# Small expert slots of a mixture of experts in plain float32, in two column tiles, alternating with full slots

## The chip, the cores and the metric

The kernel runs on one core of one Trainium2 chip. Its time is the device time of one execution in microseconds (us), a median over runs. A profile is one execution taken by the hardware profiler; its times count from the start of the profiled span. TensorE (PE) multiplies and transposes, with a separate stream of weight loads (PEld); VectorE (DVE), ScalarE (ACT) and GpSimd (POOL) work elementwise; SyncE (SP) issues the weight transfers.

## The reference

Two transformer blocks over 512 tokens of 1024 channels. The first is a state-space mixer followed by a mixture of 32 experts; the second is attention, a recurrence and a feed-forward layer. The change lies in the mixture:

```
logits = (tok @ w_router + b_router)
top_logit, top_idx = lax.top_k(logits, TOP_K)            # 4 of 32 experts a token
...
gu = xe @ w_gate_up[e] + b_gate_up[e]                    # [tokens, 1024] x [1024, 2048]
gate = jnp.minimum(gu[:, :D_FF], 7.0)
up = jnp.clip(gu[:, D_FF:], -7.0, 7.0)
act = (up + 1.0) * gate * jax.nn.sigmoid(1.702 * gate)
y = act @ w_down[e] + b_down[e]                          # [tokens, 1024] x [1024, 1024]
```

Each expert gets the tokens that chose it, 64 on average (512 x 4 / 32), and each result is weighted and added to its token's row. All is float32.

## The kernel before

The program runs `mixer`, then `moe` (L1168 to L1439), then `block2`. In `mixer`'s tail, `router` computes the choices, and sorts experts 2 to 31 by their number of tokens into 32 slots. A slot is one expert with a fixed room: 64 tokens (`HALF`, slots 2 to 13), 256 (`DOUBLE`, slots 14 and 23), or 128 (a full slot). Slots 0 and 1 hold experts 0 and 1. What no room covers would go to a loop for extra blocks at the end of `moe`.

The slots run in the order of their numbers. For each, `up` is the first product (eight raw buffers of 1 MB with 128 rows of weights each), `swiglu` the nonlinearity, and `down` the second product (four buffers). The second product of a slot runs after the first product of the next slot, so that the nonlinearity has time. `transposed` turns the tokens or hidden rows (L1233 on TensorE) and splits the result into two halves (L92).

A weight passes through three engines. SP loads it (`W.load`, or L1343 for the second product) into one of 13 raw buffers. `W.part` splits it, 1024 columns at a time: ScalarE casts it to a rounded upper half `whi` (L86), VectorE subtracts that for the lower half `wlo` (L87). TensorE multiplies three times (`mm3`, L99, L100, L101): upper by upper, lower by upper, upper by lower, all float32r. A raw buffer is free when the subtraction has read it.

A slot's tokens come by an indirect transfer that POOL issues (L1239), and its results leave by ScalarE's scaling (L1325, L1318 in a double slot), POOL's multiplication (L1326) and an indirect scatter that adds (L1327); the last slot uses VectorE (L1321) instead of the two.

Which instruction stands where on an engine is decided by a scheduler that simulates a timeline, and by explicit rules (`issue_after`). Each engine executes in that order.

Two other places matter for reading the trace. `mod_rest` (L515, in the mixer) multiplies raw weights in plain float32, four matmuls side by side in tiles of 32 array columns. L669 multiplies in plain float32 in tiles of 64 columns, first one and then the other.

Of the kernel before, what the change touches and what calls it, by code (L numbers as in the profile page):

```python
# [8 lines left out]
F32 = mybir.dt.float32  # L9
# [35 lines left out]
class Split:  # L45
    """Streams weights: raw float32 chunks, and exact float32r halves of their parts."""
# [50 lines left out]
def mm3(nc, out, a, b, first, last):  # L97
    """a, b: halves of the stationary and the moving operand"""
# [5 lines left out]
# pools whose buffers a new tile takes over without waiting for the neighbours  # L104
# [3 lines left out]
class Kernel:  # L108
# [12 lines left out]
    def behind(self, ins):  # L121
        """what is issued under this follows the given instructions on their engines"""
# [27 lines left out]
    def brow(self, pool, src, o, n, name):  # L150
        """a row of DRAM on every partition"""
# [4 lines left out]
    def rinv(self, out, src, scale, bias):  # L156
        """out = 1 / sqrt(src * scale + bias), wide"""
# [5 lines left out]
    def rsqrt(self, pool, out, src, scale, bias, n, eng=None):  # L163
        """out = 1 / sqrt(src * scale + bias) for [P, n] with a small n, by Newton's iteration"""
# [17 lines left out]
    def softplus(self, out, x, e, u, l, eng):  # L182
        """log(1 + exp(x)) = max(x, 0) + log1p(exp(-|x|)); e, u, l: scratch"""
# [6 lines left out]
        # where u rounds to 1, log1p(e) is e itself  # L190
# [8 lines left out]
    # ------------------------------------------------------------------ block 1: mixer  # L199
    def mixer(self):  # L200
# [38 lines left out]
        # --- normalised x and ctx, channels on partitions; modulation vectors  # L239
        with ExitStack() as s0:  # L240
# [50 lines left out]
            # x is turned while the modulation's weights come in  # L291
# [44 lines left out]
        # the convolution's silu is x' (1 + tanh x') with x' = x / 2  # L336
# [9 lines left out]
        def proj(raw, with_ctx, split=False):  # L346
            """psum tiles of 128 output columns; raw: weights, or their halves"""
# [10 lines left out]
        def decays(tp, px, pc, scr):  # L358
            """dt, and the decays of both directions: forward heads on 32 partitions, backward on the next"""
# [45 lines left out]
        # --- decays and Fourier mixing  # L405
# [57 lines left out]
        # x, then ctx, between zeros  # L463
# [7 lines left out]
        def tokens(x, b):  # L471
            """a block of 128 tokens of a convolution's output"""
# [20 lines left out]
        def gate(i):  # L493
            """two tiles of the gates (1 + tanh, twice the sigmoid): first of the Fourier path, then of the scan's"""
# [13 lines left out]
        def mod_rest(half):  # L508
            """rows of the modulation for the residual gates and the second norm"""
# [8 lines left out]
            def rows32(src, o, n):  # L518
                """512 columns on each 32 partitions"""
# [7 lines left out]
            if half == 0:  # L527
                # the mix is held twice as large
# [24 lines left out]
        def group_tables(B, C):  # L553
            """B with tokens on partitions, and the masked C B^T of the chunks"""
# [28 lines left out]
        # a pair of heads' own work is interleaved with the projections of the next pair  # L583
# [8 lines left out]
        for p in range(16):  # L592
# [4 lines left out]
            # x with tokens on partitions, weighted by dt and by dt * decay to the chunk's end  # L597
# [15 lines left out]
            # decays within the chunks  # L613
# [19 lines left out]
            # chunk states, carried forward and backward  # L633
# [30 lines left out]
            # within the chunks  # L664
# [7 lines left out]
            # from the states before the chunks  # L672
# [28 lines left out]
            # projections of the next group, gates, rows of the modulation  # L701
# [28 lines left out]
        # the mix, by halves of the tokens  # L730
# [5 lines left out]
        # the logits are those of x1 / rms: with the second norm's weights in the router's, its shift in the bias  # L736
# [75 lines left out]
    def bias_parts(self, src, dst):  # L812
        """three bfloat16 parts, whose sum is src, of all experts' biases: on 32 partitions each"""
# [59 lines left out]
    def recurrence_constants(self, tp):  # L873
        """half of 8 log sigmoid(lambda) and all of it, and half the biases of the gates"""
# [10 lines left out]
    # ------------------------------------------------------------------ block 1: mixture of experts  # L885
    def router(self, mx, keep, xT, ahead, st, stp):
        """The mixer's output projection, h2 and the choices of experts. keep: a pool that outlives this."""
# [10 lines left out]
        # first, for the experts' tokens come to lie here  # L898
# [23 lines left out]
        def normed(b, pw, c):  # L922
            """x1 and h2 of a block"""
# [48 lines left out]
        def picked(b):  # L972
            """the first expert's tokens, transposed, are taken from h2 by a product"""
# [194 lines left out]
    def moe(self, mx):  # L1168
# [162 lines left out]
        def act_T(act):  # L1331
            return transposed(act, 1.0 / 1.702)
# [657 lines left out]
```

## Time and profile before

| what | value |
|---|---|
| median of 3 runs | 3072.28 us (3068.34 to 3073.09) |
| span of the profiled execution | 3071.3 us |
| TensorE busy | 2964.1 us (97%) |
| VectorE busy | 2292.2 us (75%) |
| ScalarE busy | 1738.8 us (57%) |
| mean DMA rate | 210 GB/s |

The profiled execution's own time is given only as its span. Busy means that an instruction of that engine is running. The stretches of the mixture were cut at the first matmul of certain slots: slots 0 and 1, then twelve small ones, a double with its two followers, six full, a double with two, five full, and the last slot.

### The profile page before, as it was taken

The numbers are of one execution on the slowest core, as the hardware profiler recorded it, in microseconds if no ns is written. First come the engines' busy times: TensorE is split into PE (matmuls) and PEld (weight loads), VectorE is DVE, ScalarE is ACT, GpSimd is POOL, SyncE is SP. The second block draws the span as 40 slices with busy tenths as digits, with TensorE's granted clock in tenths as the row PEclk, the third lists the DMA queues.
The fourth block names the chain that finished last, engine by engine and source line by source line (L and its number), as shares of the span: only waits on it lengthen the run. The fifth ranks groups of instructions, "written<-read, shape, count | busy, mean of one in ns | idle before, by whom it ended". The sixth has DMA issues, their size and how long they took to land. (4 is left out here: it accounts for less than half of the span.)

```text
span 3071.3 us, 40680 instructions
## 1 busy us (share of the span) xinstructions
PE 2964.1 (97%) x15088; PEld 2319.1 (76%) x15088; DVE 2292.2 (75%) x2968; ACT 1738.8 (57%) x2288; POOL 431.2 (14%) x375
## 2 busy tenths in 40 slices
PE   5999999999998999999999999999969999999999
PEld 3888888788776655555677787777768888788887
DVE  4637877787769999999789997899967777843322
ACT  4444545455444777777567775677745666632221
POOL 1211121122112111111021110211130000100000
PEclk9999999999998999999999999999989999999999
DMA  8244373644747898999779997799742212443331
GB/s 217 87 121 120 107 223 127 208 139 126 216 185 289 315 344 336 342 347 347 264 258 363 367 353 252 293 369 363 264 135 79 79 52 83 158 110 96 96 103 62
DMA packets 302602, 644.62 MB, mean 210 GB/s; under 512 B 18849, under 2 KB 190513, under 8 KB 268640
## 3 DMA queue, kind: packets, MB, share of 16 engines
q1 hardware_dynamic: 275744, 569.77, 52.1%
q0 software_dynamic: 24672, 67.93, 8.2%
q10 hardware_dynamic: 1984, 4.28, 0.4%
q8 instruction: 120, 1.97, 0.3%
q14 instruction: 82, 0.67, 0.1%
HBM read 618.85 MB, written 35.21 MB: 213 GB/s over the span
## 5 line engine op out<-in xcount | busy, mean ns | idle before, releaser
L87 DVE TENSOR_TENSOR wlo<-wraw,whi 128x1024 fp32r<-128x1024 f32 x1016 | 1274.4, 1277 | 439.1 <-ACT whi L86 426.2
L86 ACT CAST whi<-wraw 128x1024 fp32r<-128x1024 f32 (+1 forms) x1019 | 1058.5, 1046 | 791.7 <-PE pg L101 231.3
L99 PE MATMUL px<-hThi,whi 128*128 128x512 f32 x576 | 231.6, 404 | 0.0
L101 PE MATMUL px<-hThi,wlo 128*128 128x512 f32 x576 | 227.3, 395 | 2.5 <-DVE wlo L87 2.5
L100 PE MATMUL px<-hTlo,whi 128*128 128x512 f32 x576 | 228.0, 396 | 0.0
L1326 POOL TENSOR_TENSOR y<-y,g2b 128x1024 f32<-128x1024 f32 (+1 forms) x33 | 87.4, 2652 | 945.2 <-ACT y L1325 864.5
L100 PE MATMUL pg<-wlo,T0h 128*128 128x512 f32 (+1 forms) x416 | 167.7, 403 | 2.9 <-DVE wlo L87 2.2
L99 PE MATMUL pg<-whi,T0h 128*128 128x512 f32 (+1 forms) x416 | 165.3, 397 | 0.0
L101 PE MATMUL pg<-whi,T0l 128*128 128x512 f32 (+1 forms) x416 | 163.9, 394 | 0.0
L100 PE MATMUL pg<-wlo,T2h 128*128 128x512 f32 (+1 forms) x352 | 141.9, 403 | 1.6 <-DVE wlo L87 1.1
L100 PE MATMUL pf<-hnlo,whi 128*128 128x512 f32 (+1 forms) x384 | 142.4, 372 | 0.0
L101 PE MATMUL pf<-hnhi,wlo 128*128 128x512 f32 (+1 forms) x384 | 142.4, 372 | 0.0
L99 PE MATMUL pf<-hnhi,whi 128*128 128x512 f32 (+1 forms) x384 | 141.6, 372 | 0.0
L99 PE MATMUL pg<-whi,T2h 128*128 128x512 f32 (+1 forms) x352 | 139.6, 397 | 0.0
L484 DVE SCALAR_TENSOR_TENSOR cacc<-cr,vecs,cacc 128x770 f32<-128x770 f32 (+1 forms) x128 | 121.4, 957 | 23.1 <-ACT cacc L482 21.9
L101 PE MATMUL pg<-whi,T2l 128*128 128x512 f32 (+1 forms) x352 | 138.3, 393 | 0.0
L101 PEld LDWEIGHTS px<-hThi,wlo 128*128 128x128 f32 x576 | 109.1, 189 | 28.6 <-DVE wlo L87 3.7
L100 PE MATMUL pg<-wlo,T1h 128*128 128x512 f32 (+1 forms) x320 | 129.7, 405 | 0.8
L99 PE MATMUL pg<-whi,T1h 128*128 128x512 f32 (+1 forms) x320 | 127.7, 399 | 0.0
L101 PE MATMUL pg<-whi,T1l 128*128 128x512 f32 (+1 forms) x320 | 126.7, 396 | 0.0
L99 PEld LDWEIGHTS px<-hThi,whi 128*128 128x128 f32 x576 | 110.1, 191 | 16.1 <-issue 1.7
L100 PEld LDWEIGHTS px<-hTlo,whi 128*128 128x128 f32 x576 | 109.7, 190 | 16.2 <-issue 1.7
(614 smaller groups left out, 6831.5 us busy)
## 6 DMA issues: line engine op xcount, KB each, us to landing
wraw<-in_w_gate_up SPq DMA_DIRECT2D x256, 1024.0 KB, 6.9
wraw<-in_w_down SPq DMA_DIRECT2D x128, 1024.0 KB, 7.0
wraw<-in_w_in SPq DMA_DIRECT2D x81, 512.0 KB, 6.3
wraw<-in_w_mod SPq DMA_DIRECT2D x23, 1024.0 KB, 8.5
wraw<-in_w_ffn_in SPq DMA_DIRECT2D x44, 512.0 KB, 5.3
wraw<-in_w_in SPq DMA_DIRECT2D x18, 1024.0 KB, 5.4
m<-acs_scr POOLq DMA_DIRECT2D x64, 256.0 KB, 5.1
wraw<-in_w_ffn_out SPq DMA_DIRECT2D x10, 1024.0 KB, 5.0
```

Of the source, the lines that this page charges most:

```text
L86: a = (copy or nc.scalar.copy)(dst[0], src)
L87: return a.ins, (eng or nc.vector).tensor_sub(dst[1], src, dst[0].bitcast(F32)).ins
L99: nc.tensor.matmul(out, a[0], b[0], start=first, stop=False)
L100: nc.tensor.matmul(out, a[0], b[1], start=False, stop=False)
L101: return nc.tensor.matmul(out, a[1], b[0], start=False, stop=last).ins
L484: nc.vector.scalar_tensor_tensor(acc, t[:, j:j + n], cw[:, j, ch:ch + 1], acc, op0=ALU.mult, op1=ALU.add)
L1326: nc.gpsimd.tensor_mul(y, y, g2b[:w])
```

## The change

Slots 2 to 15 hold 64 tokens, 14 of them, and the two doubles are slots 30 and 31, so that a slot's number is its expert's rank. A table `ORDER` sets in which order slots run. Slots of 64 tokens no longer split their weights: plain float32 matmuls take the raw buffers directly. The tokens of such a slot are gathered as half rows, [128 x 512]: partitions 0 to 63 hold the first 512 channels, 64 to 127 the second. Four transposes of 128 x 128 turn them. Two halves of the output's columns are computed by two matmuls with the same 64 stationary columns, one into PSUM partitions 0 to 63 and one into 64 to 127; the array's columns are split likewise. The nonlinearity then works on 128 x 512, and the result is scaled by ScalarE, multiplied in two halves by POOL, and scattered as half rows.

```diff
+        v4 = lambda x: x.rearrange("p b (h l) -> p b h l", h=2)
+        if half:
+            nc.vector.tensor_tensor(v4(pe), self.rc[:, 0, None, None, 0:64].to_broadcast([P, NT, 2, 64]),
+                                    place[:, :, :, None].to_broadcast([P, NT, 2, 64]), op=ALU.is_equal)
+        else:
+            nc.vector.tensor_tensor(pe, self.rc[:, 0, None, :].to_broadcast([P, NT, P]),
+                                    place.to_broadcast([P, NT, P]), op=ALU.is_equal)
...
+        for j in halves:
+            nc.vector.tensor_scalar(f[:, 0, j:j + 1], f[:, 0, j:j + 1], 2.0, self.rc[:, 2, 41:42], op0=ALU.mult, op1=ALU.add)
...
-    DOUBLE = (14, 23)
-    HALF = range(2, 14)
+    DOUBLE = (30, 31)
+    HALF = range(2, 16)
+    ORDER = (0, 1, 2, 16, 3, 17, 4, 18, 30, 5, 6, 7, 19, 8, 20, 9, 21, 10, 22, 31, 11, 12, 13, 23, 14, 24, 25, 26, 27, 28,
+             29, 15)
...
+        def transposed_half(src, scale):
+            h = src[:, 512:].rearrange("p (k t) -> p k t", k=4)
+            pt = ps_t.tile([P, KD, P], F32, tag='pt', name='pt')[:, 0:4, :]
+            for k in range(4):
+                nc.tensor.transpose(pt[:, k, :], src[:, k * P:(k + 1) * P], self.ident)
+            nc.scalar.activation(h, pt, AF.Copy, scale=scale)
+            return h
+        def half_mm(out, xT, k, ws, first, last):
+            a = xT[:, k % 4, 64 * (k // 4):64 * (k // 4) + 64]
+            for h, w in enumerate(ws):
+                nc.tensor.matmul(out[64 * h:64 * h + 64], a, w, start=first, stop=last, skip_group_check=True)
+        def half_bias(out, selT, cs):
+            for h, c in enumerate(cs):
+                nc.tensor.matmul(out[64 * h:64 * h + 64], selT.to_broadcast([96, 64]), bh[:, c:c + 512], start=True,
+                                 stop=False, skip_group_check=True)
+        def up_half(xT, rows, selT, step):
+            row = io3.tile([P, D], F32, tag='row', name='act')
+            act = row[:, :512]
+            pg = ps_g.tile([P, 4, 512], F32, tag='pg', name='pg')
+            for i in range(2):
+                half_bias(pg[:, i, :], selT, (D * i, D * i + 512))
+            for k, raw in enumerate(rows):
+                for i in range(2):
+                    half_mm(pg[:, i, :], xT, k, (raw[:, 2 * i, :], raw[:, 2 * i + 1, :]), False, k == KD - 1)
+                step(k)
+            g = one.tile([P, 2, 512], F32, tag='g', name='g')[:, 0, :]
+            nc.vector.tensor_scalar_min(g, pg[:, 0, :], 7.0)
+            nc.scalar.activation(g, g, AF.Silu, scale=1.702)
+            nc.vector.tensor_scalar(act, pg[:, 1, :], -7.0, 7.0, op0=ALU.max, op1=ALU.min)
+            nc.vector.scalar_tensor_tensor(act, act, 1.0, g, op0=ALU.add, op1=ALU.mult)
+            return row
+        def down_half(aT, rows, selT, dest, step=None):
+            tok, wgt = dest
+            y = io3.tile([P, D], F32, tag='row', name='y')[:, :512]
+            pd = ps_d.tile([P, 2, 512], F32, tag='pd', name='pd')[:, 0, :]
+            half_bias(pd, selT, (2048, 2560))
+            for c, raw in enumerate(rows):
+                for t in range(2):
+                    k = 2 * c + t
+                    half_mm(pd, aT, k, (raw[:, 2 * t, :], raw[:, 2 * t + 1, :]), False, k == KD - 1)
+                if step is not None:
+                    step(c)
+            nc.scalar.activation(y, pd, AF.Copy, scale=wgt)
+            for h in range(2):
+                q = slice(64 * h, 64 * h + 64)
+                nc.gpsimd.tensor_mul(y[q], y[q], g2b[q, 512 * h:512 * h + 512])
+            nc.gpsimd.indirect_dma_start(out=halfrows(self.x1_d), out_offset=bass.IndirectOffsetOnAxis(ap=tok, axis=0),
+                                         in_=y, in_offset=None, bounds_check=2 * S - 1, oob_is_err=False,
+                                         compute_op=ALU.add)
...
-        for e in range(NE):
-            two = e in self.DOUBLE
+        for turn, e in enumerate(self.ORDER):
+            two, half = e in self.DOUBLE, e in self.HALF
+            en = self.ORDER[turn + 1] if turn < NE - 1 else None
...
+            selT = sel[:, e:e + 1] if e > 1 else self.sel01[:, e:e + 1]
+            if half:
+                acts = [up_half(xTs[0], up_rows(wu), selT, up_step)]
+            else:
+                acts = up(xTs, up_rows(wu, two) if turn else rows0, selT, up_step, () if turn else parts0)
             if prev is not None:
-                down(aT, *prev[1:], down_step)
+                if prev[4]:
+                    down_half(aT[0], *prev[1:3], prev[3][0], down_step)
+                else:
+                    down(aT, *prev[1:4], down_step)
             else:
                 down_step(1)
...
-        down([act_T(a) for a in prev[0]], *prev[1:], tail=True)
+        down_half(act_T(prev[0][0], True), *prev[1:3], prev[3][0])
```

The router loses six small VectorE operations that moved the doubles to slots 14 and 23 (not shown).

On ScalarE, in the steady run of small slots before, 16 casts stand between the silu of one slot (L1251) and the next, with the turning of tokens (L92) and the output's scaling (L1325) between casts:

```order
L92 ACTIVATE T1h<-pt 128x8x64
L86 CAST whi<-wraw 128x1024 x16
L1251 ACTIVATE g<-g 64x1024
L86 CAST whi<-wraw 128x1024 x4
L92 ACTIVATE T2h<-pt 128x8x64
L86 CAST whi<-wraw 128x1024 x2
L1325 ACTIVATE y<-pd,slotf_8539 64x1024
```

Now, where a small slot follows a full one (L1310 is the full slot's silu, L1279 the small one's, L1253 evicts its turned rows):

```order
L86 CAST whi<-wraw 128x1024 x10
L1310 ACTIVATE g<-g 128x1024
L1295 ACTIVATE y<-pd,slotf_9573 128x512
L92 ACTIVATE T0h<-pt 128x1024
L92 ACTIVATE T1h<-pt 128x1024
L1279 ACTIVATE g<-g 128x512
L86 CAST whi<-wraw 128x1024 x2
L1253 ACTIVATE act<-pt 128x512
```

Between the full slot's silu and the small slot's, no cast stands any more; the casts of the full slot's second product come after the small slot's silu.

On TensorE, in the first product of such a small slot, the turning of the full slot's hidden rows (L1236) and the biases of its second product stand among the new matmuls (L1260):

```order
L1260 MATMUL pg<-wraw,xg_8246 64x512 x4
L1236 MATMUL pt<-ident,xg_7501 128x128 x8
L1304 LDWEIGHTS esel
L1304 MATMUL pd<-bh,esel 128x512
L1304 LDWEIGHTS esel
L1304 MATMUL pd<-bh,esel 128x512
L1260 MATMUL pg<-wraw,xg_8246 64x512 x20
```

Then the full slot's second product begins:

```order
L1304 MATMUL pg<-bh,esel 128x512
L1252 MATMUL pt<-ident,act 128x128 x4
L99 MATMUL pd<-whi,T2h 128x512
L100 MATMUL pd<-wlo,T2h 128x512
L101 MATMUL pd<-whi,T2l 128x512
```

Ahead of the split weights stand four biases of the next first product (the last of them is the first row here) and the turning of the small slot's hidden rows, for which its nonlinearity must be done.

## Rows read from the trace of the kernel before

**Rows 1.** The page's first part: busy time, share of the span, instructions.

```profile
PE 2964.1 (97%) x15088; PEld 2319.1 (76%) x15088; DVE 2292.2 (75%) x2968; ACT 1738.8 (57%) x2288; POOL 431.2 (14%) x375
```

**Rows 2.** Windows of the mixture: us, busy PE, PEld, DVE, ACT, POOL, clock, DMA share, GB/s.

```profile
958.00:1026.70 68.70, 62.98 (x304) 47.55 (x304) 64.32 (x101) 41.23 (x41) 14.63 (x8) 0.90 0.72 262
1026.70:1475.30 448.60, 446.47 (x2092) 252.95 (x2092) 427.41 (x457) 331.71 (x335) 74.66 (x37) 1.00 0.91 343
1475.30:1627.00 151.70, 148.18 (x680) 112.06 (x679) 118.07 (x116) 91.82 (x92) 27.24 (x11) 1.00 0.72 263
1627.00:1847.70 220.70, 220.44 (x1005) 176.13 (x1004) 210.41 (x175) 172.68 (x170) 37.51 (x19) 1.00 0.96 359
1847.70:1997.90 150.20, 146.81 (x657) 115.48 (x656) 114.00 (x97) 89.81 (x90) 24.80 (x11) 1.00 0.75 270
1997.90:2181.30 183.40, 183.14 (x831) 146.02 (x830) 175.25 (x146) 143.76 (x141) 27.19 (x13) 1.00 0.96 364
2181.30:2238.50 57.20, 55.69 (x246) 43.64 (x245) 51.48 (x43) 40.49 (x40) 11.40 (x4) 1.00 0.55 172
```

**Rows 3.** Waits of the DMA queue, 1627.0 to 1847.7: us in total, times, longest.

```profile
SPq L61 <- DVE wlo L87: 110.5, 48, 4.0
SPq L1343 <- DVE wlo L87: 67.8, 24, 4.2
```

**Rows 4.** Timeline of TensorE in a small slot: start, duration, instruction.

```profile
1217.50 0.40 PE L101 MATMUL pd<-whi,T0l 128*64 128x512 f32 x1
1217.73 0.39 PE L99 MATMUL pd<-whi,T0h 128*64 128x512 f32 x1
1218.05 0.71 PE L1233 MATMUL pt<-ident,act 64*128 64x64 f32 x8
1218.69 0.45 PE L100 MATMUL pd<-wlo,T0h 128*64 128x512 f32 x1
```

**Rows 5.** Timeline of TensorE, 408 to 432: plain float32 in four column tiles.

```profile
409.16 2.78 PE L515 MATMUL pm<-wraw,sc 128*32 128x512 f32 x24
...
424.35 1.06 PE L515 MATMUL pm<-wraw,sc 128*32 128x512 f32 x8
```

**Rows 6.** Windows of L669 alone: one 64-column tile, then both; columns PE, PEld.

```profile
263.40:263.80 0.40, 0.40 (x6) 0.40 (x5) 1.00 0.00 0
264.56:264.96 0.40, 0.40 (x10) 0.40 (x9) 1.00 0.00 0
```

**Rows 7.** Groups by line and shape, 1050 to 2200: count, busy us, mean ns, idle before.

```profile
L87 DVE TENSOR_TENSOR wlo<-wraw,whi 128x1024 fp32r<-128x1024 f32 x695 | 869.4, 1280 | 105.4 <-ACT whi L86 99.3
L86 ACT CAST whi<-wraw 128x1024 fp32r<-128x1024 f32 x695 | 723.2, 1049 | 300.1 <-PE pg L101 201.3 <-PE pd L101 84.3 <-DVE slotf L1161 7.2
...
L1256 DVE SCALAR_TENSOR_TENSOR act<-act,g 128x512 f32<-128x512 f32 x8 | 5.1, 684 | 0.0
L1318 ACT ACTIVATE y<-pd,slotf 128x512 f32<-128x512 f32 x8 | 5.1, 684 | 5.2 <-PE pd L101 5.2
```

**Rows 8.** Windows with the fastest weight loads; columns as in rows 2.

```profile
945.00:958.00 13.00, 8.85 (x84) 8.26 (x82) 11.72 (x35) 3.36 (x6) 0.53 (x1) 1.00 1.03 430
2060.00:2080.00 20.00, 20.00 (x92) 15.97 (x91) 19.33 (x17) 15.45 (x15) 0.00 (x0) 1.00 1.01 404
```

**Rows 9.** Timelines of VectorE at the end, and of POOL in a full slot.

```profile
2238.57 1.28 DVE L1321 SCALAR_TENSOR_TENSOR y<-pd,slotf,g2b 128x1024 f32<-128x1024 f32 x1 [2.79 <-PE pd L101]
...
2045.01 2.38 POOL L1326 TENSOR_TENSOR y<-y,g2b 128x1024 f32<-128x1024 f32 x1 [30.49 <-ACT y L1325]
```

**Rows 10.** Windows after a stall near the mixture's start; columns as in rows 2.

```profile
982.50:985.90 3.40, 0.89 (x5) 0.71 (x5) 3.40 (x5) 0.74 (x1) 1.42 (x2) 0.99 0.51 206
985.90:989.30 3.40, 3.40 (x10) 2.40 (x8) 2.91 (x6) 1.97 (x2) 0.00 (x0) 0.50 0.84 272
```

**Rows 11.** List of DMA issues: the scatters, count, us to landing.

```profile
x_scr<-y,sloti POOLq DMA_INDIRECT x34, 7.8
```

More of the change, by code (lines that the diff above doesn't have):

```diff
@@ L1027, in router @@
                                     key[:, :, None].to_broadcast([P, NE, NE]), op=ALU.is_lt)
[L1028 to L1029 removed]
             slot = tp.tile([P, NE], F32, name='slot')
[L1031 to L1035 removed]
+            nc.vector.tensor_reduce(slot, less, axis=AX.X, op=ALU.add)
             eye = tp.tile([96, NE], F32, name='eye')
@@ L1076, in router, with table @@
         return first
-    def table(self, pool, out, place, v, first):
+    def table(self, pool, out, place, v, first, half=False):
         nc = self.nc
         pe = pool.tile([P, NT, P], BF16, tag='pe', name='pe')
-        nc.vector.tensor_tensor(pe, self.rc[:, 0, None, :].to_broadcast([P, NT, P]), place.to_broadcast([P, NT, P]),
-                                op=ALU.is_equal)
+        v4 = lambda x: x.rearrange("p b (h l) -> p b h l", h=2)
[5 more added lines that the diff above has]
+                                    place.to_broadcast([P, NT, P]), op=ALU.is_equal)
         for b in range(NT):
@@ L1146, in extra, with slots @@
         return r[:, 0, :, None], v
-    def slots(self, pool, tab, n, sfx):
+    def slots(self, pool, tab, n, sfx, halves=()):
         nc = self.nc
@@ L1235, in transposed, with gather @@
             return h
-        def gather(i, tok):
-            x = xgs[i % 2][:tok.shape[0]]
-            nc.gpsimd.indirect_dma_start(out=x, out_offset=None, in_=self.h2_d,
+        def gather(i, tok, half=False):
+            x = xgs[i % 2]
+            nc.gpsimd.indirect_dma_start(out=x[:, :D // 2] if half else x, out_offset=None, in_=halfrows(self.h2_d) if half else self.h2_d,
                                          in_offset=bass.IndirectOffsetOnAxis(ap=tok, axis=0),
-                                         bounds_check=S - 1, oob_is_err=False)
+                                         bounds_check=(2 * S if half else S) - 1, oob_is_err=False)
@@ L1329, in down, with act_T @@
                                              compute_op=ALU.add)
-        def act_T(act):
-            return transposed(act, 1.0 / 1.702)
+        def act_T(act, half=False):
+            return (transposed_half if half else transposed)(act, 1.0 / 1.702)
         def down_rows(w, two=False):
@@ L1350, in reg @@
             return nc.values_load(ap, engines=[mybir.EngineType.SP], min_val=0, max_val=NE - 1)
-        blocks = [(s_, j) for s_ in range(NE) for j in ((0, P) if s_ in self.DOUBLE else (0,))]
+        blocks = [(s_, j) for s_ in self.ORDER for j in ((0, P) if s_ in self.DOUBLE else (0,))]
         at = lambda e: [i for i, b in enumerate(blocks) if b[0] == e]
@@ L1367, in step @@
                         nc.vector.tensor_scalar_add(src, self.rm[:, :, e:e + 1], -float(o))
-                    self.table(io, ptab[:, j, :], src, self.V[:, :, e, :], j == 0)
+                    self.table(io, ptab[:, j, :], src, self.V[:, :, e, :], j == 0, e in self.HALF)
                 if j == n - 1:
-                    t = self.slots(keep, ptab, n, str(i0))
+                    t = self.slots(keep, ptab, n, str(i0), [i for i in range(n) if blocks[i0 + i][0] in self.HALF])
                     for i in range(n):
-                        w = P // 2 if blocks[i0 + i][0] in self.HALF else P
-                        tabs.append([x[:w, i:i + 1] for x in t])
+                        tabs.append([x[:, i:i + 1] for x in t])
             return step
@@ L1388, in moe @@
                 wu, wdn = dyn(wgu, r), dyn(wd, r)
-            if 0 < e < NE - 1:
-                for i in at(e + 1):
-                    xgs_[i] = gather(i, tabs[i][0])
-            i0 = 2 * e + 2 if e else 0
-            tab = tables(i0, min(2 if e else 4, nb - i0)) if i0 < nb else None
+            if turn and en is not None:
+                for i in at(en):
+                    xgs_[i] = gather(i, tabs[i][0], en in self.HALF)
+            i0 = 2 * turn + 2 if turn else 0
+            tab = tables(i0, min(2 if turn else 4, nb - i0)) if i0 < nb else None
             aT, xn = [], []
@@ L1414, in moe @@
             xTs = xn
-            prev = (acts, down_rows(wdn, two), sel[:, e:e + 1] if e > 1 else self.sel01[:, e:e + 1], [tabs[i] for i in at(e)])
-        down([act_T(a) for a in prev[0]], *prev[1:], tail=True)
+            prev = (acts, down_rows(wdn, two), selT, [tabs[i] for i in at(e)], half)
+        down_half(act_T(prev[0][0], True), *prev[1:3], prev[3][0])
         W.rings = ring
```

22 lines of the change are left out of this document (8 added, 14 removed).

## The prediction

> **What bounds the kernel now.** I read the page's busy shares first, then windows cut at the slots of the mixture of experts, then the waits, then single matmuls. TensorE is busy for 97% of the span [rows 1], so a shorter time needs less work on it or the same work in fewer passes. The mixture lasts from 958.0 to 2238.5 us, 1280.5 of 3071.3 us [rows 2]. Its second stretch is twelve slots of 64 tokens, 448.60 / 12 = 37.4 us each; the fourth and sixth are full slots, 220.70 / 6 = 36.8 and 183.40 / 5 = 36.7 us; TensorE is busy for over 99% of each at a clock of 1.00. So a slot with half the tokens costs as much as a full one: the time goes with the columns of weights that stream through the array, and 64 rows leave half of the array's columns empty. The reader is to see that nothing else limits yet, though much is close: VectorE is busy for 95% of the fourth stretch, the DMA share is 0.96, and yet the DMA queue waits, for buffers that VectorE's subtraction has still to read [rows 3]. Weights wait for room; TensorE does not wait for weights.
>
> **The change on TensorE.** Removed per small slot: three float32r matmuls for each of 48 products of 512 columns (eight blocks of rows by four of columns in the first product, eight by two in the second), one every 0.23 us, as successive starts show [rows 4]: 33.1 us. Added: 48 plain float32 matmuls, in 24 pairs, one half of the columns in array columns 0 to 63, the other in 64 to 127. The trace has no such pair with weights. It has the next thing: plain float32 on raw weights in four tiles of 32 columns, L515, where a buffer's four matmuls leave eight records, two each. 24 records take 2.78 us and 8 take 1.06 [rows 5], so 16 more take 1.72, which is 0.43 us for each pass of four tiles over 512 columns; a product has two such passes. If the tiles run beside each other, a pair costs 2 x 0.43 = 0.86 us; if in turn, 1.72. That is the range of the disputed price, 20.6 to 41.3 us for the 24 pairs. I take 0.86, because L515's four tiles share a pass, and because the one place with two 64-column tiles in plain float32, L669, has six records in 0.40 us where one tile works and ten where both do [rows 6]. To that come three pairs of bias matmuls (3 x 0.23 = 0.7) and eight transposes: 64 rows wide they take 1218.69 - 1218.05 = 0.64 us for eight [rows 4], 128 wide at most twice that, so 0.9. A change of shape leaves some 0.1 us (0.32 instead of 0.23 between starts, [rows 4]); with about ten to a pair of slots plus what follows them that is 1.5. Small slot: 20.6 + 0.7 + 0.9 + 1.5 = 23.7 us instead of 37.4.
>
> The Trainium skill, "TensorE: Matmul & The Clock Gate", Part 3, speaks against a full doubling: three column tiles gave 2.38 times the work, not three. By that efficiency, 0.79 a tile, two tiles would give 1.59 times, a pair of products 1.08 us, and the end would be some 45 us later than my sum; L515's sixteen records in 1.72 us show no such loss [rows 5].
>
> **A wait that comes instead.** The casts on ScalarE and the subtractions on VectorE vanish for small slots. Their silu does not, and the order shows it ahead of the casts of the full slot whose second product comes next. So at the nine places where the order goes from a 64-token slot to a full one, TensorE waits for VectorE's minimum, the silu, a cast and a subtraction: about 0.68 + 0.68 for 128 x 512 (by the rows of that shape), 1.05 and 1.28, together 3.7 us [rows 7]. Queued behind the waiting matmul are the rest of that second product and the next first product. Bias matmuls, transposes and the first third of a block fill some 1.35 us, so 2.4 is lost. From both sides: 0 if casts run ahead anyway, 3.7 if nothing fills. I take 2.4. A pair of a small and a full slot is thus 23.7 + 2.4 + 36.8 = 62.9 us of TensorE, against 74.2.
>
> **The transfers.** Every slot still loads its 12 buffers of 1 MB. What TensorE saves, the DMA must deliver sooner. In the fourth stretch a slot moves 359 GB/s x 36.8 us = 13.2 MB. The fastest stretch of weight loads moves 430 GB/s for 13 us, and inside the sixth 404 for 20 us with the share at 1.01 [rows 8]. By 430, a slot needs 30.7 us and a pair 61.4; by the share, with 1.00 as its end, 0.96 x 36.8 = 35.3 and 70.6 [rows 2]. Both bounds straddle TensorE's 62.9, so transfers and TensorE become limits together. The middle is 66.0, and I add 1 us for waits in which neither covers the other: 67 a pair. The twelve megabytes of a small slot come faster than they can, those of the full one slower; thirteen raw buffers even that out over a pair, as the order alternates.
>
> **What lies off the path.** Gathers, half as many transposed columns to evict, two small POOL multiplications for one large, and one tiny VectorE operation per small slot hide behind TensorE. Without that cover the POOL pair costs about 2.4 us a slot, as the one now does [rows 9]. The router loses six tiny VectorE operations; under 1 us, taken as 0. At the end the last slot is a small one, and its output goes by ScalarE (0.68) and POOL (2.38, by the one large multiplication that it splits) where VectorE's 1.28 stood [rows 7, 9]; the rest of POOL's start makes it +1.6.
>
> **The sum.** The first two slots stay: 68.7. Seven pairs alternate (2/16, 3/17, 4/18, 8/20, 9/21, 10/22, 14/24): 7 x 67 = 469. Two groups hold a double slot, three small and one full. A double's surplus is read from stretch three, 151.70 for a double and two full slots: 151.7 - 2 x 36.8 = 78.1, and from five 150.2 - 73.5 = 76.7, so 77; a group is 77 + 3 x 23.7 + 36.8 + 2.4 = 187.3 (its transfers, 5 x 35.3 = 176.5, fit inside), two are 374.6. Slots 25 to 29: 5 x 36.7 = 183.5. The end, now 57.2 with two full second products and a first, becomes 42: a small first product 14.5, a full second 12.3 (a third of 36.8), a small second 7.4, and 8 for waits, as 57.2 less 4/3 of 36.8 leaves now. Together 1137.8 against 1280.5: -142.7, with the end's +1.6 -141.1. The profiled execution's span is 3071.3; the median of the runs shown, 3072.28, lies 1.0 above, which I take as what surrounds a span. 3071.3 - 141.1 + 1.0 = 2931 us. With pairs at 63 (TensorE alone) it is 2903, at 70.6 it is 2956.
>
> **Rivals.**
> A, the transfers stay slow, and the clock dips. If the DMA gives no more than the 364 GB/s of the sixth stretch [rows 2], a pair takes 26.4 MB / 364 = 72.5 us, 7 x 5.5 = +38. TensorE then waits in every small slot, and after such a wait the trace has a clock of 0.50 for the next 3.4 us [rows 10], which loses 1.7; one dip per small slot is 14 x 1.7 = +24. 2992 us. For it: 13.2 MB a slot at a share of 0.96. Against: 404 and 430 GB/s [rows 8], and that the queue was kept waiting by buffers [rows 3]. The Trainium skill, "DMA: Bandwidth & Descriptors", section "Where 436 GB/s comes from", takes this side: HBM limits a core to some 358 GB/s, by which a pair would take 73.8 us; its own measured table has 425 for one core alone, and the trace's 430 agrees with that.
> B, waits hide. If the casts run ahead and the transfers reach 430 GB/s, a pair is 61 us and a group 185: 7 x 6 + 2 x 2.3 = 47 less, 2884.
> C, slower: the two tiles take turns. A pair of products is 1.72 us, a small slot 41.3 + 3.1 = 44.4, a pair of slots 44.4 + 2.4 + 36.8 = 83.6, a group 249.4, the end 63 (28.3 + 12.3 + 14.4 + 8): 68.7 + 585 + 499 + 183.5 + 63 = 1399, +119, with the end's 1.6 and the 1.0 about 3193. It decides from about 36 us a small slot, 1.37 us a pair of products. For it: both tiles read the same stationary rows, and no row has exactly this pair. Against: [rows 5, 6].
> D, it does not do what it says: a 64-token slot gets an expert with more, and the loop for extra blocks runs, which no block needs now (34 blocks for 32 slots and two doubles, [rows 11]). One block alone would cost about the 57.2 us of the last slot: 2990. The fourteenth smallest expert has 63 tokens by the router's choices, so one token decides.
>
> **How the numbers follow.** Forecast 55%, A 20, B 15, C 5, D 3, and 2 for tiles that overlap just enough to change nothing. The range 2880 to 3005 takes B's end, and A and D; beyond it lie C and mishaps. Runs of this kernel spread 0.15%, so 0.2% (6 us) is about what can be told from no change. Faster 0.93 (all but C and the rest), the same 0.02, slower 0.05.
>
> **What would show it.** In the profile after: the four records of a pair of products in 0.86 us (if in 1.72, C); a small slot near 24 us; DMA over a pair at 390 GB/s or more (if 360 with TensorE waiting for raw weights and a clock under 1.00, A); the queue's waits for VectorE's subtraction mostly gone; TensorE waiting 2 to 3 us for the subtraction after each small slot's last first-product matmul; 34 scatters, as now. The prediction is wrong if the small slots stay above 30 us, or if time outside 958 to 2238 us changes by more than a few us.

## The result and the profile after

The changed kernel takes 2943.73 us (median of 4 runs, 2940.44 to 2948.37) against 3070.31 us for the kernel before in the same comparison. The ratio is 0.9594, with a 95% interval from 0.9578 to 0.9610: 127 us faster, where 141 were forecast. The profiled execution has a span of 2946.6 us against 3071.3, 124.7 us less; it is the longest of the four runs, 4.6 us above their median.

The page's first part of the changed kernel, to be held against [rows 1]:

```profile
PE 2798.5 (95%) x14304; PEld 2124.7 (72%) x14304; DVE 1857.2 (63%) x2611; ACT 1380.0 (47%) x1953; POOL 423.3 (14%) x390
```

TensorE lost 166 us of work and the span 125, so its share fell from 97 to 95%: some of the gain went into waits. VectorE lost 435 us and ScalarE 359; neither was the limit in the kernel before.

Windows of the mixture in the changed kernel, with the columns of [rows 2]. The stretches are slots 0 and 1, three pairs, the first group with a double, three pairs, the second group, one pair, slots 25 to 29, and the end:

```profile
958.20:1026.80 68.60, 61.97 (x303) 46.67 (x305) 65.91 (x97) 41.59 (x41) 18.24 (x8) 0.90 0.73 267
1026.80:1231.30 204.50, 197.10 (x926) 118.44 (x922) 132.34 (x164) 97.83 (x102) 35.83 (x22) 1.00 1.00 389
1231.30:1427.40 196.10, 186.71 (x850) 111.44 (x852) 95.99 (x126) 65.22 (x71) 35.80 (x19) 0.99 0.82 313
1427.40:1623.40 196.00, 184.82 (x863) 111.59 (x860) 119.92 (x125) 95.61 (x99) 33.54 (x22) 1.00 1.02 404
1623.40:1816.70 193.30, 187.18 (x840) 112.79 (x838) 85.38 (x76) 67.55 (x74) 34.36 (x21) 0.98 0.84 322
1816.70:1884.10 67.40, 61.99 (x282) 36.94 (x281) 38.88 (x34) 31.67 (x34) 11.75 (x9) 1.00 1.02 409
1884.10:2070.40 186.30, 180.49 (x809) 141.20 (x807) 175.63 (x144) 141.28 (x138) 29.17 (x14) 1.00 1.00 388
2070.40:2112.70 42.30, 38.21 (x164) 19.64 (x163) 12.77 (x13) 11.33 (x12) 7.86 (x4) 0.96 0.57 178
```

The sum is 1154.5 us against 1280.5 before and 1137.8 forecast. Stretch by stretch, measured and forecast: 68.6 and 68.7; seven pairs 204.5 + 196.0 + 67.4 = 467.9 and 469; two groups 389.4 and 374.6; five full slots 186.3 and 183.5; the end 42.3 and 42. Nearly all of the 16.7 us missing lies in the two groups with a double slot. The pairs of the fourth stretch run at a DMA share of 1.02 and 404 GB/s, which looks like a limit; TensorE's waits below show that it is none there.

One caution on stretches: those before start at a slot's first bias matmul, these at its first matmul with weights. In the kernel before, the two lie 6 us apart, and 9.6 us at slot 14 (1475.28 and 1484.90), so a single stretch compares to some us only. The sums are free of this.

Timeline of TensorE in one pair of a small and a full slot in the changed kernel (start, duration, instruction; in brackets what it waited for):

```profile
1426.99 0.62 PE L1264 MATMUL pg<-bh,esel 96*64 96x512 bf16 x4 [1.32 <-DVE act L1313]
...
1435.76 8.80 PE L1260 MATMUL pg<-wraw,xg 128*64 128x512 f32 x40
1445.96 1.04 PE L1304 MATMUL pg<-bh,esel 96*128 96x512 bf16 x4 [1.39 <-DVE act L1280]
...
1448.28 0.50 PE L100 MATMUL pd<-wlo,T0h 128*128 128x512 f32 x1 [0.58 <-DVE wlo L87]
```

Forty records of the new matmuls take 8.80 us, so a pair of products with its four records takes 0.88. The turn out of the small slot has two waits: the four biases of the next full product wait 1.39 us for VectorE's clip of the small slot (L1280), which still reads the PSUM tile they go to, and then L100 waits 0.58 for the lower half. At the turn into the small slot, the same happens with the full slot's clip (L1313), 1.32 us.

TensorE's longest waits in the three pairs of the fourth stretch (us in total, times, longest):

```profile
PE pg L1304 <- DVE act L1280: 4.2, 3, 1.4
PE pg L1264 <- DVE act L1313: 2.7, 2, 1.3
PE pd L100 <- DVE wlo L87: 1.7, 3, 0.6
```

With three shorter groups they are 11.2 us, 8.2 of them for clips, and none for a transfer; casts and subtractions wait 1.2 us for transfers there.

The queue's waits in the same three pairs, against [rows 3]:

```profile
SPq L61 <- DVE wlo L87: 39.0, 18, 4.1
SPq L61 <- PE pg L1260: 33.9, 19, 3.1
SPq L1402 <- DVE wlo L87: 18.1, 10, 2.7
SPq L1402 <- PE pd L1260: 15.6, 8, 3.4
```

The queue still waits for buffers, now also for TensorE, which reads raw buffers itself. Weights are ahead of their use, even here.

In the doubles, the wait lies halfway, where the second half of the columns takes over the PSUM tile. Timeline of TensorE at that place, first before, then after (group one, and group two):

```profile
1509.83 1.09 PE L1233 MATMUL pt<-ident,xg 128*128 128x128 f32 x8
1511.86 0.59 PE L1245 MATMUL pg<-bh,esel 96*128 96x512 bf16 x2 [0.94 <-DVE act L1254]
```

```profile
1258.41 0.59 PE L1304 MATMUL pg<-bh,esel 96*128 96x512 bf16 x2 [2.06 <-DVE act L1313]
...
1652.65 1.09 PE L1236 MATMUL pt<-ident,act 128*128 128x128 f32 x4 [3.30 <-DVE act L1315]
```

And windows over the same places of the changed kernel (columns as in [rows 2], the clock is the third number from the end):

```profile
1256.00:1260.00 4.00, 1.94 (x8) 1.22 (x7) 4.00 (x5) 2.04 (x2) 0.00 (x0) 0.87 0.21 86
1260.00:1264.00 4.00, 4.00 (x14) 3.23 (x13) 0.69 (x2) 0.57 (x1) 0.00 (x0) 0.70 0.77 262
...
1652.00:1656.00 4.00, 3.35 (x10) 2.66 (x11) 1.80 (x3) 0.00 (x0) 1.36 (x1) 0.50 0.85 321
1656.00:1660.00 4.00, 4.00 (x14) 3.11 (x14) 0.00 (x0) 0.77 (x1) 0.00 (x0) 0.71 0.34 75
```

Before, eight transposes of the next slot's tokens happened to stand at this point and covered a microsecond; now biases of two matmuls (group one), or four transposes that the scheduler put ahead of what they need (group two). After the longer waits the clock is at 0.50 (1.2 GHz) for part of the next windows, where it stayed at 1.00 after the 0.94 us before. The length of the wait alone does not tell: after one of 2.25 us, ahead of the first product of slot 3 (to 1100.16), it stayed at 1.00 too. A window of the kernel before behind its 0.94 us, and one of the changed kernel behind its 2.25:

```profile
1512.00:1516.00 4.00, 4.00 (x18) 3.19 (x17) 2.15 (x3) 0.68 (x1) 0.24 (x1) 1.00 0.58 197
```

```profile
1103.00:1107.00 4.00, 4.00 (x20) 1.26 (x18) 1.75 (x2) 0.00 (x0) 0.00 (x0) 1.00 1.03 424
```

From the start of its first matmul with weights to that of its last, the double's first product takes 51.7 and 55.3 us instead of 48.6 and 48.8 (before, counted from the second matmul, as the first stands alone inside the product ahead). Waits of 1.00 and 0.53 us behind its first matmul are in the new figures.

### The profile page after: what moved, and what is told of

The parts are those of the page before. It is cut to its first block, busy times and chain, and to the rows that moved or that the text cites. A ratio compares the mean times of both kernels' runs of the same rounds, so it can differ in the third digit from the quotient of the medians.

```text
span 2946.6 us, 37902 instructions
## 1 busy us (share of the span) xinstructions
PE 2798.5 (95%) x14304; PEld 2124.7 (72%) x14304; DVE 1857.2 (63%) x2611; ACT 1380.0 (47%) x1953; POOL 423.3 (14%) x390
## 4 chain that ended last, share of the span: by engine, by line
PE 42%; issue 5%; DMA 3%; DVE 3%; ACT 2%; POOL 1%; ACTq 0%; POOLq 0%; DVEq 0%; SPq 0%
PE pg L1260 4%; PE pf L99 3%; PE pf L101 3%; PE pf L100 3%; PE pd L1260 2%; PE pg L100 2%; PE px L100 2%; PE pg L99 2%; PE pg L101 2%; PE px L99 2%; PE px L101 2%; DMA wraw<-in_w_gate_up 1%; PE pfo L101 1%; PE pfo L100 1%; PE pfo L99 1%
## 5 line engine op out<-in xcount | busy, mean ns | idle before, releaser
L87 DVE TENSOR_TENSOR wlo<-wraw,whi 128x1024 fp32r<-128x1024 f32 (+1 forms) x680 | 851.0, 1271 | 458.8 <-ACT whi L86 448.1
L86 ACT CAST whi<-wraw 128x1024 fp32r<-128x1024 f32 (+1 forms) x683 | 705.7, 1044 | 684.7 <-PE pg L101 156.2
L100 PE MATMUL px<-hTlo,whi 128*128 128x512 f32 x576 | 228.0, 396 | 0.0
L1260 PE MATMUL pg<-wraw,xg 128*64 128x512 f32 x896 | 207.2, 596 | 3.4 <-ACT xg L1253 1.8
L1260 PEld LDWEIGHTS pg<-wraw,xg 128*64 128x64 f32 x896 | 63.1, 136 | 119.3 <-issue 108.9
L100 PE MATMUL pf<-hnlo,whi 128*128 128x512 f32 (+1 forms) x384 | 142.4, 372 | 0.0
L99 PEld LDWEIGHTS px<-hThi,whi 128*128 128x128 f32 x576 | 110.0, 191 | 16.2 <-issue 1.7
L100 PEld LDWEIGHTS px<-hTlo,whi 128*128 128x128 f32 x576 | 109.8, 191 | 16.2 <-issue 1.7
L100 PE MATMUL pg<-wlo,T1h 128*128 128x512 f32 x256 | 105.0, 410 | 4.5 <-DVE wlo L87 4.5
L1260 PE MATMUL pd<-wraw,act 128*64 128x512 f32 x448 | 105.0, 598 | 0.0
L99 PE MATMUL px<-h2hi,whi 128*128 128x512 f32 x256 | 103.9, 406 | 0.0
L99 PE MATMUL pg<-whi,T1h 128*128 128x512 f32 x256 | 103.4, 404 | 0.0
L100 PE MATMUL px<-h2lo,whi 128*128 128x512 f32 x256 | 102.8, 402 | 0.0
L101 PE MATMUL pg<-whi,T1l 128*128 128x512 f32 x256 | 101.8, 398 | 0.0
L101 PE MATMUL px<-h2hi,wlo 128*128 128x512 f32 x256 | 100.7, 393 | 0.0
```

Of the source, the lines that this page charges most:

```text
L99: nc.tensor.matmul(out, a[0], b[0], start=first, stop=False)
L100: nc.tensor.matmul(out, a[0], b[1], start=False, stop=False)
L101: return nc.tensor.matmul(out, a[1], b[0], start=False, stop=last).ins
L1260: nc.tensor.matmul(out[64 * h:64 * h + 64], a, w, start=first, stop=last, skip_group_check=True)
```

## The experiments

Theory P: the column tiles halve TensorE's passes, TensorE sets the time, and turns and doubles lost the rest. Rival T: transfers set the pairs, as the forecast had it. All times are medians; the kernel before had 3069 to 3071 us beside them.

**The same tile.** Both column halves go to the first 64 array columns.

```diff
-                nc.tensor.matmul(out[64 * h:64 * h + 64], a, w, start=first, stop=last, skip_group_check=True)
+                nc.tensor.matmul(out[0:64], a, w, start=first, stop=last, skip_group_check=True)
```

> The second half of the columns is multiplied into the same 64 array columns and PSUM rows as the first, so the output is not the reference's; all else stays. If the two tiles work beside each other (0.86 us a pair of products), the 24 pairs of a small slot now cost 1.72 each, 20.6 us more a slot, 14 x 20.6 = +288, less up to 40 that waits for weights and stalls give back: 3190 to 3232 us. If the gain came from raw float32 without the split alone, the time stays at 2944.

Measured: 3199.03 us (one run). Timeline of TensorE in a small slot of it:

```profile
1534.91 8.75 PE L1260 MATMUL pg<-wraw,xg 128*64 128x512 f32 x20
1543.87 8.80 PE L1260 MATMUL pg<-wraw,xg 128*64 128x512 f32 x20
```

Twenty records take what forty took: the two tiles do twice the work. The kernel is 255 us slower than the changed one and 128 us slower than before. Raw float32 without the second tile is thus a loss; the rival with tiles in turn was priced at 3193. The Trainium skill, "TensorE: Matmul & The Clock Gate", Part 3, has 2.38 for three column tiles; for two tiles with 512 columns the loss against the ideal that it suggests isn't there.

**The order alone.** The new order and number of small slots, but small slots split and multiply as before.

```diff
-            two, half = e in self.DOUBLE, e in self.HALF
+            two, half = e in self.DOUBLE, False
```

(with the gather, the tables and the last slot of the kernel before)

> The new order and the new numbers of slots (14 small), but small slots split their weights and multiply as before. If the alternation by itself is worth nothing while TensorE passes the same columns: 14 x 37.4 + 16 x 36.8 + 2 x 77 and the ends, as before, 3060 to 3085 us. If a part of the gain came from the order (small and full slots in turn), 3020 to 3050.

Measured: 3077.88 us, ratio 1.0029 (1.0018 to 1.0041). The order and the two further small slots without the new matmuls are worth nothing, and cost some 9 us; the new arithmetic is worth 134.

**Half of the transfers.** Small slots load 512 of every 1024 columns and use them twice.

```diff
-                    half_mm(pg[:, i, :], xT, k, (raw[:, 2 * i, :], raw[:, 2 * i + 1, :]), False, k == KD - 1)
+                    half_mm(pg[:, i, :], xT, k, (raw[:, i, :], raw[:, i, :]), False, k == KD - 1)
```

(likewise in the second product, with loads of 0.5 MB)

> Small slots load half of the columns of every weight buffer and use it for both halves, so the output is not the reference's; instructions stay on all engines but the transfers of a small slot shrink from 12.6 to 6.3 MB. If TensorE sets a pair of slots (65.4 us measured) the time stays within 2934 to 2944. If the transfers set it, a pair falls to TensorE's own 62.9 or less and the full slots 25 to 29 from 37.3 to 36.7: 2915 to 2925.

Measured: 2944.05 us, ratio 0.9588 (0.9573 to 0.9602), no change. Windows over the three pairs of the fourth stretch and over slots 25 to 29 of it:

```profile
1432.60:1630.00 197.40, 190.04 (x866) 111.80 (x863) 126.34 (x126) 94.94 (x98) 41.18 (x24) 0.99 0.87 321
1890.60:2066.10 175.50, 175.40 (x797) 139.83 (x797) 166.22 (x138) 136.79 (x134) 25.88 (x13) 1.00 0.93 345
```

With 321 GB/s instead of 404 the three pairs take 197.4 us instead of 196.0. But this is not the same kernel with fewer bytes: the scheduler ordered anew and now puts a small slot's second product among the full slot's first. Over the mixture TensorE is idle for 36.4 us instead of 56.0 and busy for 1114.2 instead of 1098.5, with the clock at 0.50 in more places. So the equal total does not show that the transfers cost nothing. What speaks against T in the pairs is this window together with the changed kernel's own waits, none of them for a transfer.

Slots 25 to 29 are another matter: 175.5 us without a wait, instead of 186.3. In the changed kernel the chain of work that ended last passes there through transfers for 30 us (start, us, what):

```profile
1895.57 17.86 DMA wraw<-in_w_gate_up
1913.55 12.24 DMA wraw<-in_w_down
```

So behind the last pair the transfers may cost some us; the new order keeps this run from showing it.

**Small slots in a row.**

```diff
-    ORDER = (0, 1, 2, 16, 3, 17, 4, 18, 30, 5, 6, 7, 19, 8, 20, 9, 21, 10, 22, 31, 11, 12, 13, 23, 14, 24, 25, 26, 27, 28,
+    ORDER = (0, 1, 2, 3, 4, 5, 6, 7, 8, 9, 10, 11, 12, 13, 14, 30, 16, 17, 18, 19, 20, 21, 22, 31, 23, 24, 25, 26, 27, 28,
```

> Thirteen small slots in a row, then the full ones with the two doubles among them. If transfers limit a run of small slots, one takes 13.2 MB / 404 GB/s = 32.7 us instead of TensorE's 23: 13 x 32.7 + 14 x 36.7 + 2 x 78 + 68.6 + 42 = 1205 for the mixture instead of 1154.5, so about 2995 us, with TensorE waiting for raw weights and a clock below 1.00 there. If TensorE alone sets the time and the transfers follow, nothing is lost and fewer turns from small to full give 10 to 20 us: 2925 to 2935.

Measured: 2964.04 us, ratio 0.9655 (0.9641 to 0.9670). (A small slot directly ahead of a double has its tokens overwritten by the double's gather, so slot 14 computes with others; its work is the same.) Window over three neighbouring small slots, and the two largest of TensorE's waits:

```profile
1190.90:1285.10 94.20, 75.63 (x358) 22.37 (x356) 17.91 (x37) 7.53 (x12) 15.72 (x13) 1.00 1.02 413
```

```profile
PE pg L1260 <- DMA wraw<-in_w_gate_up: 36.6, 57, 1.4
PE pd L1260 <- DMA wraw<-in_w_down: 10.3, 18, 1.2
```

Here the transfers do set the time: 31.4 us a slot at 413 GB/s, where the same slot needs 23.1 us in the changed kernel's runs of three. Neither expectation was right: 20 us slower, not 51. Slots 5 and 6 take only 25.6 and 25.9 us, the rate is 413 and not 404, and eight turns fewer give something back; how much each is worth was not measured. The clock stayed at 1.00; no single wait was over 1.4 us. The Trainium skill, "DMA: Bandwidth & Descriptors", section "Where 436 GB/s comes from", says that some 358 GB/s of HBM bind such loads; on one core alone 413 over 94 us contradict it, and its table's 425, for a core alone, lies near.

**All in pairs.** Every small slot stands alone, in 14 runs instead of ten.

```diff
-    ORDER = (0, 1, 2, 16, 3, 17, 4, 18, 30, 5, 6, 7, 19, 8, 20, 9, 21, 10, 22, 31, 11, 12, 13, 23, 14, 24, 25, 26, 27, 28,
+    ORDER = (0, 1, 2, 16, 3, 17, 4, 18, 30, 5, 19, 6, 20, 7, 21, 8, 22, 31, 9, 23, 10, 24, 11, 25, 12, 26, 13, 27, 14, 28,
```

> The same slots, but every small slot has full slots or a double beside it: no run of three small slots, no run of five full ones. If TensorE's work sets the time wherever weights come early enough, the sum is the same, with two us for each of some four turns more, and the full slots lose the 0.6 us each that they ran over before: 2940 to 2955. If the runs of three small slots were what the groups lost, about 15 us come back: 2930.

Measured: 2969.20 us, ratio 0.9670 (0.9655 to 0.9685): 25 us slower, a miss of both. Window over two pairs of it:

```profile
1854.70:1985.00 130.30, 122.25 (x555) 72.94 (x554) 75.69 (x64) 61.59 (x64) 21.77 (x14) 1.00 1.02 404
```

A pair takes 65.2 us here as there. In the changed kernel two small slots in the middle of a run take 46.3 us (1735.27 to 1781.58), 23.1 each, and a full one 36.8 [rows 2], together 59.9. So 5.3 to 5.5 us of a pair are its two turns, waits and changes of shape together, and four runs more cost 25 us, 6 each.

**Twelve small slots.** Slots 14 and 15 become full.

```diff
-    HALF = range(2, 16)
+    HALF = range(2, 14)
```

(and in `ORDER`, slots 14 and 15 stand where 13 and 14 stood, and 13 comes last)

> Twelve small slots instead of 14; two slots among the groups and pairs are full. If a small slot costs 23 to 23.7 us against 36.8, each is worth 13 to 13.8 and, with the turn it adds, some 12: 2944 + 24 to 28 = 2968 to 2972 us. If transfers set the pairs, a full slot in a group is partly hidden: under 2960.

Measured: 2966.74 us, ratio 0.9658 (0.9636 to 0.9681), with runs from 2956.71 to 2971.61: 23 us for two slots and one run fewer. By 36.8 - 23.1 = 13.7 each, less one run's turns of 5, 22 was to be expected; it agrees within the spread of the runs, and lies just under the first of the two expected ranges.

**One PSUM tile.** The first products' tile is made once.

```diff
-            pg = ps_g.tile([P, 4, 512], F32, tag='pg', name='pg')
+            pg = pgs
```

> One PSUM tile for all first products instead of a new one each time, so that the biases of the next product wait only for the instruction that has read their own banks (the minimum) and not for the clip behind it; the order on TensorE stays. If the 20.4 us that TensorE waits for the clip, and the clock of 0.50 to 0.71 behind the long waits in the doubles, are lost time, 8 to 16 us come back: 2928 to 2936. If the next wait (for the lower halves) takes their place, nothing: 2941 to 2944.

Measured: 2946.44 us, ratio 0.9598 (0.9585 to 0.9611), no change. The edit did not do what it was to do. TensorE's waits in it (the clips are L1280 and L1315, L1313 of the changed kernel):

```profile
PE pg L1304 <- DVE act L1280: 7.9, 7, 1.4
PE pg L1264 <- DVE act L1315: 6.2, 4, 2.2
PE pg L1304 <- DVE act L1315: 5.4, 3, 2.1
```

They are those of the changed kernel to 0.1 us: the biases still wait for the clip, which reads other banks of the same tile, so this says nothing on what the wait is worth.

**Two PSUM tiles.** One for the gates, one for the rest.

```diff
+        def pg_pair():
+            return [ps_g.tile([P, 2, 512], F32, tag=t, name=t) for t in ('pga', 'pgb')]
...
-            pg = ps_g.tile([P, 4, 512], F32, tag='pg', name='pg')
+            pg = pg_pair()
```

> The first products' PSUM tile is two tiles, one for the gates and one for the rest, so that the biases of the next gates wait for the minimum alone; the scheduler may order anew. If the waits for the clip (20.4 us in all) and the low clock behind those in the doubles are what the two groups with doubles lost against the prediction (15 us), 8 to 16 us come back: 2928 to 2936. If something else comes last there, or the new order loses as much, 2940 to 2950.

Measured: 2939.20 us, ratio 0.9575 (0.9562 to 0.9588). TensorE's waits for the readers of these tiles (the minimum is L1312):

```profile
PE pga L1304 <- DVE g L1312: 2.4, 1, 2.4
...
PE pgb L1304 <- DVE act L1280: 2.2, 6, 0.8
PE pgb L1304 <- DVE act L1316: 2.0, 2, 1.3
...
PE pgb L1264 <- DVE act L1316: 1.4, 3, 0.5
```

The waits for the readers fall from about 20 to about 8 us, and the first product of the first double from 51.7 to 48.8 us (its halfway wait is gone), that of the second from 55.3 to 52.4. The medians differ by 4.5 us, with intervals that overlap. It is the fastest version found, by a hair; by its profile, the doubles lost some 6 us to this wait, not all 15.

**Five runs.** If turns cost 5.5 us, fewer runs should pay.

```diff
-    ORDER = (0, 1, 2, 16, 3, 17, 4, 18, 30, 5, 6, 7, 19, 8, 20, 9, 21, 10, 22, 31, 11, 12, 13, 23, 14, 24, 25, 26, 27, 28,
+    ORDER = (0, 1, 2, 3, 4, 16, 17, 18, 30, 5, 6, 7, 8, 19, 20, 21, 22, 31, 9, 10, 11, 12, 23, 24, 13, 14, 25, 26, 27, 28,
```

> The same slots with the small ones in five runs (three, four, four, two, one) instead of ten. If every run of small slots costs TensorE about 5.5 us at its two turns (a pair measured 65.4 us against some 60 for its parts without turns; four runs more cost 25 us, eight fewer saved what transfers then took), five fewer give 27: 2917 us, up to 2926 where transfers fall behind within a run of four. If instead transfers set the time of a run from its second slot on (31.3 us a small slot instead of 23), the eight slots behind a run's first cost more than after's four did, some 30 us come on top, and nothing is won: 2940 to 2950.

> The five runs with the two PSUM tiles. If the waits for the clip are of the turns' cost, fewer turns leave less of them and the two tiles give under 4.5 us more: 2912 to 2917. If they are of the doubles, the same 4.5 as before: 2912. If the scheduler's new order takes it back, 2917 to 2925.

Measured: 2949.86 us, ratio 0.9615 (0.9602 to 0.9628), and with the two tiles 2963.90 us, ratio 0.9660 (0.9645 to 0.9676). Nothing is won. The first time lies in the range of the second expectation, but not by its mechanism: two small slots in the middle of a run of four take 45.5 us (1676.20 to 1721.70), 22.8 each and not 31.3. With the two tiles, which had gained 4.5 us in the other order, it is 14 us slower than without, a miss for which no cause is known.

Two of TensorE's waits in the five runs, and a window over a full slot beside another:

```profile
PE pg L100 <- DVE wlo L87: 15.4, 17, 1.9
...
PE pg L99 <- ACT whi L86: 6.7, 6, 2.0
```

```profile
1448.40:1488.80 40.40, 39.04 (x184) 30.08 (x183) 39.72 (x42) 28.53 (x28) 5.98 (x4) 1.00 1.02 412
```

Over the mixture, TensorE's waits for the clips fall from 20.4 to 10.0 us, as fewer turns should have it, but its waits for upper and lower halves rise from 16.2 to 25.7. Full slots side by side take 40 us instead of 36.8, with VectorE busy for 39.72 of 40.40; one reading is that VectorE has no room there for the tables of later slots. The rows do not bear it out: that work adds up to 17.4 us in the full slots of either order, and TensorE is itself busy for 39.04 of the 40.40, with eight transposes and eight table matmuls more than a plain full slot has. Why the halves come later is open.

**Subtractions on GpSimd**, a try at that reading: two of sixteen in the first product of each full slot.

```diff
-                                                              nc.gpsimd if pre and h and k in (3,5,7) else None)
+                                                              nc.gpsimd if h and k in ((3, 5, 7) if pre else (2, 6)) else None)
```

> The five runs, and in every full slot two of the sixteen subtractions of the first product go to GpSimd (2.97 us each there by the trace) instead of VectorE (1.25). If VectorE is what holds the neighbouring full slots at 38 to 40 us (39.72 busy of 40.40 in one, with the tables of later slots among its work), 2.5 us less of it bring some eight such slots back towards TensorE's 36.8: 2930 us. If transfers hold them (412 GB/s at a share of 1.02 there), the time stays at 2946 to 2953. If GpSimd's 2.97 us come too late for TensorE, it rises over 2955.

> The order of the changed kernel with the two PSUM tiles (2939.2 us), and the same two subtractions of every full slot on GpSimd. If VectorE holds the three full slots at 38 to 40 us near the end and the full halves of some pairs, 5 to 10 us come back: 2929 to 2934. If GpSimd is late, a microsecond or more is lost in each of 16 full slots: 2950 or more.

Measured: 2963.65 us, ratio 0.9654 (0.9641 to 0.9667), and 2962.74 us, ratio 0.9656 (0.9643 to 0.9669): 14 and 24 us slower than without. In the first, GpSimd's subtractions and TensorE's longest wait:

```profile
L87 POOL TENSOR_TENSOR wlo<-wraw,whi 128x1024 fp32r<-128x1024 f32 x33 | 89.3, 2706 | 169.2 <-ACT whi L86 159.0 <-DVE val L1111 5.4 <-issue 4.0
```

```profile
PE pg L100 <- DVE wlo L87: 27.9, 28, 3.2
```

A subtraction takes 2.71 us there, and TensorE uses up a half of a buffer in six matmuls of 0.23. It waits only 2.8 us for GpSimd's own halves; its waits for VectorE's rise from 15.4 to 27.9 us. So the trial took work from VectorE and lost time, which speaks against VectorE as the bound and does not settle it: the order changed too. That VectorE bounds neighbouring full slots is not shown.

## Why the prediction was right, and where it failed

- The work on TensorE was sized rightly. A pair of products was put at 0.86 us and takes 0.88; a small slot at 22.2 without its changes of shape, and takes 23.1 within a run. That two tiles share a pass, read from four narrow tiles [rows 5] and two short windows [rows 6], held: the same tile for both halves doubles the time. The rival with tiles in turn did not come about, but its price, 3193, is near what the same tile cost, 3199.
- The pairs came out at 66.8 us on average (467.9 / 7) against 67, for a wrong reason. So the agreement is luck. The step that failed is "the middle is 66.0", the transfers as the limit of a pair: in three pairs at 404 GB/s TensorE waits 11.2 us, none of it for a transfer, and with half the bytes in small slots three pairs take 197.4 us instead of 196.0. TensorE's own sum, 62.9, was too small instead: the small slot's work was 0.9 us more, and where the sum counted 2.4 us of waits and 1.5 of shape changes, together 3.9, the turns take 5.3 to 5.5. Both together make the 65.3 us of these pairs. The bounds for the transfers were sound: 413 GB/s in a steady row of small slots lies between 35.3 us (share) and 30.7 (430 GB/s) a slot, at 31.4.
- The added wait was there, in another form. The forecast had the chain of minimum, silu, cast and subtraction, 2.4 us. The row shows 1.39 us for the clip, since the next first product's biases stand ahead, and 0.58 for the subtraction: 2.0. It left out the other turn, into the small slot, with 1.32.
- The doubles were taken as unchanged, 77 us; here the forecast lost its 15 us. It did not look for what covered their halfway wait. The order had changed around them, the cover went, and the clock fell behind the longer waits: over the two first products it is 0.97 and 0.94 on average, which by itself is an estimated 1.6 and 3.3 us (the missing share of the two times). The two PSUM tiles give back 2.9 us of each first product. What the rest of the groups lost isn't split up. The 77 us also hung on where the stretches were cut: from first matmul with weights to first matmul with weights the two stretches before are 148.1 and 149.6 us (1484.90 to 1632.95, 1854.18 to 2003.82), a surplus of 74.5 and 76.1.
- Full slots at the end ran 0.6 us longer each (2.8 in all), which the forecast took as unchanged; TensorE waits 5.8 us for lower halves there. The end and the path through ScalarE and GpSimd came out as counted: 42.3 us against 42, and the span fell 1.3 us less than the mixture, against 1.6.
- Rival A failed in both parts: between slot 2 and slot 29 TensorE waits for raw weights once, 1.7 us, and the clock is low in the doubles alone. Rival D too: there are 34 scatters as in [rows 11]. B's hidden waits did not happen.

## What to carry to other kernels

With 64 stationary columns, two column tiles in plain float32 on unsplit weights beat three split matmuls on half of the array here (0.88 us for two products against 6 x 0.23 = 1.38), and spare two engines their work; without the second tile it is a loss. A DMA share of 1.02 does not say whether transfers bind: it stood beside no wait for a transfer in the pairs, and beside waits of up to 1.4 us for about half of the buffers in the row of small slots. Look at what TensorE waits for before believing the share, and when a trial changes the order too, compare waits and stretches, not the total alone. After a reordering, look at each wait that the old order covered by chance, for it is not in the table of old waits.

## What the runs showed of the hardware that was not expected

Two 64-column tiles gave a factor of 2.0 (forty records in 8.80 us, twenty in one tile in 8.75), with no loss for sharing. One core sustained 413 GB/s of 1 MB loads for 94 us. A share of 1.02 at 404 GB/s stood beside no wait of TensorE for a transfer. Waits of 0.94 and 2.25 us left the clock at 1.00, and after waits of 2.06 and 3.30 us it was at 0.50 for part of the following 8 us: the length of one wait did not decide it.
